# A two-layer hybrid backbone step on one core: loads of the start, modulation steps, the last RWKV pair and the odd projection's operands in another order

## Chip, cores and metric

The kernel runs on one core of a Trainium2 chip. The metric is the device time of one execution in microseconds (us).

## What is computed

The program is one inference step of a diffusion backbone of two layers, on 256 prompt tokens and 1024 sample tokens, 1024 features wide. Every sub-layer is a norm with a shift and a scale, a mixer or an MLP, and a gated addition to x. The shifts, scales and gates (the modulation) are one product per layer of the two conditioning vectors with `mod_w`. The cut reference:

```python
def modulation(cond, w, b):            # per layer, 6 x 1024 columns
    return silu(cond) @ w + b          # shift, scale, gate of mixer and of MLP
for l in range(2):
    h = rmsnorm(x, norm_mix[l]) * (1 + scale) + shift
    if l == 0:   # gated DeltaNet (q, k, v after a conv and silu) beside a gated short conv
        y = concat(gdn(h), short_conv(h)) @ ev_w_out
    else:        # windowed attention with sinks beside RWKV-7, forwards and backwards
        y = concat(attention(h), rwkv(h)) @ od_w_out
    x = x + gate * y
    h = rmsnorm(x, norm_mlp[l]) * (1 + scale2) + shift2
    x = x + gate2 * (relu(h @ mlp_w1) ** 2 @ mlp_w2)
out = rmsnorm(x, norm_final)
# end of the RWKV head, per pair of heads:
#   (groupnorm(y) * ln_w + ln_b + sum(r * k * r_k) * v) * g
```

## The kernel before

All activations lie feature by token: x is 8 tiles of 128 features by 1280 tokens. A dense product keeps fp32 accuracy through a split of both operands into a high and a low part (`split`: the high part on ACT, L247; the low part on POOL, L251, or on DVE, L253) and three TensorE products for each 128 by 128 block (`dense_mm`, L275). A column block of 128 outputs goes over the tokens in three chunks, CHUNKS = 256, 512 and 512 tokens wide, and over 8 feature blocks, so one chunk takes 24 matmuls. `load_w` loads a weight column block into a `raw` buffer (SP's queue, L263) and splits it into `whl`.

A scheduler with its own model of time sets the order in which each engine runs its instructions; the code below gives it the dependences. `late(a, b)` adds a dependence without a semaphore: a stands behind b in the order. `paced` does the same for matmuls that are to fill gaps of a serial chain. A DMA is issued by the queue of SP, ACT or POOL in that queue's order, and at most eight lanes are in use: a DMA waits for the lane that was given out eight DMAs earlier.

The places that matter here:

- **Start** (end of `tile_kernel`). `load_vec(1, SY, const)` loads eight small parameter rows on SP's queue (L185), among them the conditioning vectors, from which `scp` is made (L292 to L294). `load_x` loads the tokens on ACT's queue (L464), TensorE turns them (L151). `mod_set` (L300) loads 32 pieces of `mod_w` on SP's queue (L304), multiplies them (L305) and turns the result (L312). `norm` makes hhi and hlo (L454, L455). `spill_x` writes x to device memory (L126), eight DMAs on SP's queue.
- **Even mixer.** `qkv(h, i)` is one dense column block with a conv, a tanh (L619) and, for k and q, squares (ACT L630, POOL for the prompt) whose sums TensorE makes (L635). After each chunk `go_on(3)` takes three steps of the layer's other 16 groups of modulation columns: ACT multiplies a loaded piece (L357), POOL adds (L361), DVE folds (L367), TensorE sums the partitions (L373). The order was `qkv(0, 1)`, the small column block `ba` (L702, L711), then `qkv(0, 0)` and `qkv(0, 2)`.
- **MLP 0.** Layer 1's modulation is made beside the MLP, on DVE (L350).
- **Odd mixer.** Eight units of RWKV (four pairs b of heads, two directions d), each a serial chain `recur`, are filled up with attention items; `prep` of the next unit (its buffers come from the pool `rmore` on some turns, L1575) and `finish` of the pair before are spread over the same slot. `finish` has five parts: load r and the two k (L1806), mean and variance of Y (L1808 to L1818), the bonus (L1819, L1820), v and g (L1822, L1823), turn Y (L1827), sum the bonus (L1829), affine (L1831), gate (L1835) and write to `sp_w` (L1838). For the last pair all of it stands behind the last chain.
- **Odd projection.** `unspill_x` loads x in 24 DMAs on ACT's queue (L131). `odd_out` loads eight operands of 128 by 1280 (four of attention from `sp_a`, four of RWKV from `sp_w`) into two buffers `a` (L1849), and splits them; `project` runs the dense blocks db 7 to 4, chunk by chunk, then 3 to 0, and adds to x (L1866).

## Time and profile before

| | |
|---|---|
| Median of 3 runs | 4275.2 us (4267.73 to 4288.86) |
| Profiled execution, its own time | 4277.4 us |
| Its span, first to last instruction | 4275.4 us |
| Busy: PE, DVE, ACT, POOL | 3933.8, 2285.1, 1285.4, 1300.8 us |
| Mean granted TensorE clock | 0.944 of full speed |
| Stages (starts): start, even mixer, MLP 0, odd mixer, projection, MLP 1 | 0, 69, 1010, 1900, 3184, 3376 us |

PE is busy for 92% of the span; it is idle for the other 341 us. A wait is read with the engine that had it, the line that waited and the releaser: "PE pm L635 <- ACT t L630: 12.7" says that TensorE stood 12.7 us before its product of line 635, until ACT had written t at line 630.

### The profile page before, as it was taken

To read this page: it belongs to the slowest core of one execution; us is meant where nothing else is said; L and a number is where in the kernel's file an instruction comes from. 1 tells how busy PE (TensorE), PEld (TensorE's weight loads), DVE (VectorE), ACT (ScalarE), POOL (GpSimd) and SP (SyncE) were. 2 spreads that over 40 slices of the span, in tenths; PEclk is the share of its full clock that TensorE was granted. 3 is DMA by queue.
4 is the path that set the end of the run, shared out by engine and by line. 5 is a ranking of instruction groups with operands and counts; after the bars stand their busy time and mean duration, and the time that the engine had idled before them with its cause. 6 is when DMAs were issued, how large, how long until landed. Compare 5 with 4: busy or idle time off the path is not lost. (4 is left out here: it accounts for less than half of the span.)

```text
span 4275.4 us, 68726 instructions
## 1 busy us (share of the span) xinstructions
PE 3933.8 (92%) x27295; PEld 3228.1 (76%) x27295; DVE 2285.1 (53%) x4799; ACT 1285.4 (30%) x2721; POOL 1300.8 (30%) x1139
## 2 busy tenths in 40 slices
PE   6889989998999999999889889999868899999999
PEld 3677877786888888877667667777647788888887
DVE  5377676546455555463365577778541533333335
ACT  4454543223111111143222234444321311111112
POOL 2444542224222332242432231212022323322232
PEclk8889999999999999999989889999879999999999
DMA  5323332332122222125466543333242111111111
GB/s 206 101 81 100 93 98 70 126 131 73 53 75 72 71 79 75 47 98 181 147 211 185 137 101 82 91 88 82 64 134 67 30 40 40 40 35 35 40 40 60
DMA packets 437952, 382.90 MB, mean 90 GB/s; under 512 B 125684, under 2 KB 373503, under 8 KB 437503
## 3 DMA queue, kind: packets, MB, share of 16 engines
q1 hardware_dynamic: 405802, 314.45, 25.0%
q10 hardware_dynamic: 31829, 64.06, 4.5%
q8 instruction: 215, 3.52, 0.3%
q14 instruction: 106, 0.87, 0.1%
HBM read 290.31 MB, written 88.08 MB: 89 GB/s over the span
## 5 line engine op out<-in xcount | busy, mean ns | idle before, releaser
L275 PE MATMUL pd<-hhi,whl 128*128 128x512 f32 (+1 forms) x5376 | 1538.8, 366 | 55.0 <-ACT hhi L247 25.3
L275 PEld LDWEIGHTS pd<-hhi,whl 128*128 128x128 f32 x5376 | 974.9, 193 | 213.4 <-ACT hhi L247 27.1
L275 PE MATMUL pd<-hlo,whl 128*128 128x512 f32 (+1 forms) x2688 | 986.0, 367 | 27.1 <-POOL hlo L251 13.4
L512 DVE SCALAR_TENSOR_TENSOR x<-pm,mods,x 128x512 f32<-128x512 f32 (+1 forms) x768 | 501.7, 659 | 724.9 <-PE pm L511 724.7
L251 POOL TENSOR_TENSOR whl<-raw,whl 128x1024 fp32r<-128x1024 f32 (+1 forms) x203 | 471.2, 2331 | 611.3 <-ACT whl L247 610.1
L275 PEld LDWEIGHTS pd<-hlo,whl 128*128 128x128 f32 x2688 | 518.1, 193 | 115.3 <-DVE hlo L455 19.2
L509 PE MATMUL pm<-hh,whl 128*128 128x512 f32 (+1 forms) x1536 | 545.7, 356 | 0.0
L510 PE MATMUL pm<-hl,whl 128*128 128x512 f32 (+1 forms) x1536 | 544.4, 354 | 0.0
L511 PE MATMUL pm<-hh,whl 128*128 128x512 f32 (+1 forms) x1536 | 542.9, 354 | 0.0
L498 ACT ACTIVATE t<-pd 128x512 f32<-128x512 f32 (+1 forms) x192 | 101.1, 528 | 1307.6 <-PE pd L275 1305.3
L251 POOL TENSOR_TENSOR hl<-t,hh 128x512 fp32r<-128x512 f32 (+1 forms) x192 | 217.6, 1134 | 822.5 <-DVE hh L249 802.5
L509 PEld LDWEIGHTS pm<-hh,whl 128*128 128x128 f32 x1536 | 288.9, 188 | 44.5
L510 PEld LDWEIGHTS pm<-hl,whl 128*128 128x128 f32 x1536 | 289.4, 188 | 43.5
L511 PEld LDWEIGHTS pm<-hh,whl 128*128 128x128 f32 x1536 | 289.5, 188 | 41.7
L249 DVE CAST hh<-t 128x512 fp32r<-128x512 f32 (+1 forms) x192 | 164.0, 855 | 228.4 <-ACT t L499 228.3
L247 ACT ACTIVATE whl<-raw 128x1024 fp32r<-128x1024 f32 (+1 forms) x203 | 201.7, 1011 | 162.8 <-PE pm L511 74.7
L361 POOL TENSOR_TENSOR acc<-acc,modw 128x512 f32<-128x512 f32 x112 | 152.3, 1360 | 151.9 <-ACT modw L357 132.4
L357 ACT ACTIVATE modw<-modw,scp 128x256 f32<-128x256 f32 x224 | 113.0, 506 | 67.3 <-DMA modw<-in_mod_w_dram 61.9
L1276 PE MATMUL pa<-hst,whl 128*128 128x512 f32 (+1 forms) x432 | 121.1, 380 | 9.5 <-DMA hst<-sp_h 8.5
L350 DVE SCALAR_TENSOR_TENSOR acc<-modw,scp,acc 128x512 f32<-128x512 f32 x168 | 129.1, 800 | 0.2 <-DMA modw<-in_mod_w_dram 0.2
L284 PE MATMUL pd<-hhi,whl 128*128 128x512 f32 (+1 forms) x384 | 109.2, 364 | 4.9 <-ACT hhi L247 3.0
L420 ACT ACTIVATE sq<-x 128x512 f32<-128x512 f32 (+1 forms) x120 | 66.2, 558 | 157.3 <-DVE x L1866 48.0
(388 smaller groups left out, 5989.8 us busy)
## 6 DMA issues: line engine op xcount, KB each, us to landing
raw<-in_mlp_w_dram SPq DMA_DIRECT2D x128, 512.0 KB
modw<-in_mod_w_dram SPq DMA_DIRECT2D x128, 256.0 KB
hst<-sp_h ACTq DMA_DIRECT2D x48, 512.0 KB
modw<-in_mod_w_dram SPq DMA_DIRECT2D x128, 128.0 KB
rkk<-sp_r SPq DMA_DIRECT2D x40, 384.0 KB
raw<-in_ev_w_in_dram SPq DMA_DIRECT2D x28, 512.0 KB
x_dram<-x SPq DMA_DIRECT2D x16, 640.0 KB
x<-x_dram ACTq DMA_DIRECT2D x32, 256.0 KB
```

The source lines that it names most:

```text
L247: A.activation(out=hi, in_=src, func=AF.Copy)
L249: V.tensor_copy(out=hi, in_=src)
L251: G.tensor_tensor(out=lo, in0=src, in1=hi.bitcast(F32), op=ALU.subtract)
L275: paced(PE.matmul(ps[:, :N], w, x[:, t0:t0 + N], start=(n + i == 0), stop=(n == KB - 1 and i == 2)), N / 2400)
L350: V.scalar_tensor_tensor(out=acc[:, s], in0=w, scalar=scp[:, kb, s:s + 1], in1=acc[:, s], op0=ALU.mult, op1=ALU.add)
L357: bi = A.activation(out=dst[:, s], in_=w[:, 0], func=AF.Copy, scale=scp[:, kb, s:s + 1])
L361: G.tensor_tensor(out=acc, in0=acc, in1=w, op=ALU.add)
L509: PE.matmul(ps[:, :N], wh, hh[:, b, :N], start=(b == 0), stop=False)
L510: PE.matmul(ps[:, :N], wh, hl[:, b, :N], start=False, stop=False)
L511: PE.matmul(ps[:, :N], wl, hh[:, b, :N], start=False, stop=(b == 1))
L512: V.scalar_tensor_tensor(out=xt[db][:, t0:t0 + N], in0=ps[:, :N], scalar=gate[:, db, s:s + 1], in1=xt[db][:, t0:t0 + N], op0=ALU.mult, op1 ...
L1276: burst([(lambda w_=w_, i=i, w=w, h=h: PE.matmul(st["ps"][w_][:, :N], st["w"][w_][:, w, kb, :], x[:, h, :N], start=(kb + i == 0), stop=(kb ...
```

## The change

Six things are changed.

1. The small rows of `load_vec(1)` and the making of `scp` go into `conditions()`, on ACT's queue behind the first two loads of x. SP's queue begins with `mod_w`. The eight spills of x are kept behind the last load of `mod_w`.
2. `qkv(0, 1)` and `qkv(0, 0)` both come before `ba`; `ba`'s operands get buffers of their own. The first nine calls of `go_on` take no step of the modulation, each later one takes four.
3. In MLP 0 the DVE steps of layer 1's modulation are kept behind the latest eviction of the MLP (`late`, no semaphore).
4. `prep`'s extra buffers serve turns 9, 10 and 11 of each 11 instead of 1, 2 and 3.
5. For the last RWKV pair, bonus and gate are made `ahead`, in the last unit's slot, and written to `sp_e`; `rest` loads them again and does what needs Y.
6. `odd_out` loads each operand into the place of its own low part, in the order 0, 1, 2, 4, 5, 6, 3, 7, the last in three chunks, all on SP's queue and ahead of x, and splits there. The products take the feature blocks in the same order, and for db 7 to 4 the 256 tokens of the prompt come last. `unspill_x` is gone before the projection.

```diff
-    def spill_x(xt):
+    def spill_x(xt, after=None):
         for kb in range(KB):
-            SY.dma_start(out=x_dram[kb], in_=xt[kb])
+            dma = SY.dma_start(out=x_dram[kb], in_=xt[kb])
+            if after is not None:
+                late(dma, after)
...
-    load_vec(1, SY, const)
...
+    def conditions():
+        load_vec(1, A, const)
+        V.memset(scp, 0.0)
...
+                    late(bi, state["evict"])
                     yield
...
-            def go_on(n):
-                for _ in range(n):
-                    next(steps, None)
-
-            qkv(0, 1)
-            raw = state["raw"].tile([P, KB, 16], F32, tag="raw", name="raw")
+            def go_on():
+                if next(calls) >= 9:
+                    for _ in range(4):
+                        next(steps, None)
+
+            for i in (1, 0):
+                qkv(0, i)
+            raw = ge.tile([P, KB, 16], F32, tag="D1", name="rawb", bufs=1)
...
-            for i in (0, 2):
-                qkv(0, i)
+            qkv(0, 2)
...
-                    if u >= 7:
-                        pace["used"] = max(pace["used"], start - 0)
+                if u == 7:
+                    pre, last = finish(b)
+                    slot = [f for k, f in enumerate(slot) for f in ([f, pre.pop(0)] if k % 4 == 3 and pre else [f])] + pre
+                    pace["used"] = max(pace["used"], start)
...
-                g = state["more"] if state["more"] and turn[0] % 11 in (1, 2, 3) else gp
+                g = state["more"] if state["more"] and turn[0] % 11 in (9, 10, 0) else gp
...
+            def ahead(c0):
+                vg = tp.tile([P, 3, 256], F32, tag="vg", name="vg", bufs=1)
+                for _ in bonus(c0, vg):
+                    pass
+                ps = ps_t("pa")
+                paced(PE.matmul(ps[:, 256:], C["bd"], vg[:, 1], start=True, stop=True), 0.5)
+                paced(PE.matmul(ps[:, :256], ups[:, 2, :], vg[:, 2], start=True, stop=True), 0.5)
+                V.tensor_tensor(out=vg[:, 0], in0=vg[:, 0], in1=ps[:, 256:], op=ALU.mult)
+                A.activation(out=vg[:, 1], in_=ps[:, :256], func=AF.Copy)
+                SY.dma_start(out=mid["e"][:, :, 64 * c0:64 * c0 + 256], in_=vg[:, 0:2])
+
+            def rest(c0):
...
+                SY.dma_start(out=eg[:, 0:2], in_=mid["e"][:, :, sl])
+                head_norm(Yt)
+                ps = ps_t("pa")
+                by_feature(ps, Yt)
+                affine(eg[:, 2], ps)
+                G.tensor_tensor(out=eg[:, 2], in0=eg[:, 2], in1=eg[:, 0], op=ALU.add)
+                V.tensor_tensor(out=eg[:, 2], in0=eg[:, 2], in1=eg[:, 1], op=ALU.mult)
+                SY.dma_start(out=mid["w"][b][:, sl], in_=eg[:, 2])
...
-            for j in range(KB):
-                a = gp.tile([P, T], F32, tag="a", name="a", bufs=2)
-                (SY if j % 2 else A).dma_start(out=a, in_=mid["a"][j] if j < 4 else mid["w"][j - 4])
-                split(hs[j][0], hs[j][1], a, "a", "v" if j % 2 else "g")
+            def operand(j, sl, eng_lo):
+                hi, lo = hs[j][0][:, sl], hs[j][1][:, sl]
+                dma = SY.dma_start(out=lo.bitcast(F32), in_=(mid["a"][j] if j < 4 else mid["w"][j - 4])[:, sl])
+                split(hi, lo, lo.bitcast(F32), "a", eng_lo)
+                return dma
+
+            for j in (0, 1, 2, 4, 5, 6, 3):
+                last = operand(j, slice(0, T), "v" if j in (2, 5) else "g")
+            first = SY.dma_start(out=xt[7], in_=x_dram[7])
+            late(first, last)
+            for t0, N, s in (CHUNKS[1], CHUNKS[2], CHUNKS[0]):
+                last = operand(7, slice(t0, t0 + N), "v")
+            for kb in range(KB - 2, -1, -1):
+                late(SY.dma_start(out=xt[kb], in_=x_dram[kb]), last)
...
-            project(e2, xt, hs, cols, gate, range(KB))
+            project(e2, xt, hs, cols, gate, (0, 1, 2, 4, 5, 6, 3, 7))
...
-            for c in CHUNKS:
+            for c in (CHUNKS[1], CHUNKS[2], CHUNKS[0]):
...
         load_x(xp_, xt, (2, 4))
+        conditions()
...
-        spill_x(xt)
+        spill_x(xt, state["last"])
...
-    unspill_x(xt)
     odd_out(xt, hs, mod_gate(1, 0))
```

**SP at the start, before**, from the eighth small row to the last piece of `mod_w` (L304) and the two weight loads behind it. L126 are the spills of x, L702 is the load of `ba`'s weights.

```order
L185 DMA rows_74<-in_gdn_norm_dram 1x128
L304 DMA modw<-in_mod_w_dram 128x512 x17
L263 DMA raw<-in_ev_w_in_dram 128x8x128
L702 DMA raw<-in_ev_w_in_dram 128x8x16
L304 DMA modw<-in_mod_w_dram 128x512 x8
L126 DMA x_dram<-x 128x1280 x3
L304 DMA modw<-in_mod_w_dram 128x512 x2
L126 DMA x_dram<-x 128x1280 x4
L304 DMA modw<-in_mod_w_dram 128x512 x4
L126 DMA x_dram<-x 128x1280
L304 DMA modw<-in_mod_w_dram 128x512
L263 DMA raw<-in_ev_w_in_dram 128x8x128 x2
```

The same place in the changed program, from SP's first DMA on (L308 is the load of `mod_w` now, L709 that of `ba`):

```order
L145 DMA cst<-in_c_dram 128x896
L147 DMA cst_72<-in_c_dram 128x192
L308 DMA modw<-in_mod_w_dram 128x512 x11
L263 DMA raw<-in_ev_w_in_dram 128x8x128 x2
L308 DMA modw<-in_mod_w_dram 128x512 x10
L263 DMA raw<-in_ev_w_in_dram 128x8x128
L308 DMA modw<-in_mod_w_dram 128x512 x2
L263 DMA raw<-in_ev_w_in_dram 128x8x128
L308 DMA modw<-in_mod_w_dram 128x512 x9
L126 DMA x_dram<-x 128x1280 x8
L709 DMA rawb<-in_ev_w_in_dram 128x8x16
```

No spill and no load of `ba` stands among the 32 pieces any more; one weight load more does.

**ACT in the even mixer, before**, from the first tanh of `qkv(0, 1)` (L619) to the squares (L630); L357 are the modulation's products.

```order
L619 ACTIVATE t_807<-cv 128x512
L619 ACTIVATE t_827<-cv 128x512
L357 ACTIVATE modw<-modw,scp 128x256 x2
L574 ACTIVATE raw<-pd 128x256
L575 ACTIVATE cv<-pd,vec_83 128x256
L247 ACTIVATE whl<-raw 128x1024
L357 ACTIVATE modw<-modw,scp 128x256
L619 ACTIVATE t_845<-cv 128x256
L357 ACTIVATE modw<-modw,scp 128x256 x9
L630 ACTIVATE t_863<-cv 128x512
L630 ACTIVATE t_869<-cv 128x512
```

The same in the changed program (tanh L624, squares L635, products L362):

```order
L624 ACTIVATE t_807<-cv 128x512
L624 ACTIVATE t_810<-cv 128x512
L362 ACTIVATE modw<-modw,scp 128x256 x2
L579 ACTIVATE raw<-pd 128x256
L580 ACTIVATE cv<-pd,vec_197 128x256
L247 ACTIVATE whl<-raw 128x1024
L362 ACTIVATE modw<-modw,scp 128x256
L624 ACTIVATE t_813<-cv 128x256
L635 ACTIVATE t_818<-cv 128x512
L362 ACTIVATE modw<-modw,scp 128x256
L635 ACTIVATE t_824<-cv 128x512
```

The nine products that stood right ahead of the first square are gone from there; some products still stand in this stretch, since the scheduler puts them where it finds room.

**SP at the projection, before**, from the last writes of `sp_w` on; the other four operands and the 24 loads of x are on ACT's queue.

```order
L1838 DMA sp_w<-yT 128x256
L1849 DMA a<-sp_a 128x1280
L1849 DMA a<-sp_w 128x1280 x2
L263 DMA raw<-in_od_w_out_dram 64x4x128 x2
```

The same in the changed program (L1893 is the last write of `sp_w`, L1907 the operands, L1913 and L1918 x):

```order
L1893 DMA sp_w<-eg 128x256
L263 DMA raw<-in_od_w_out_dram 128x4x128
L1907 DMA hlo<-sp_a 128x1280 x3
L1907 DMA hlo<-sp_w 128x1280 x3
L1907 DMA hlo<-sp_a 128x1280
L1913 DMA x<-x_dram 128x1280
L1907 DMA hlo<-sp_w 128x512
L1907 DMA hlo<-sp_w 128x256
L1907 DMA hlo<-sp_w 128x512
L1918 DMA x<-x_dram 128x1280 x7
```

All operands now stand in one queue, seven of them ahead of any load of x.

## Rows read from the trace of the kernel before

**Rows 1.** Stretches: us, then busy us of PE, PEld, DVE, ACT, POOL; clock, DMA share, GB/s.

```profile
0.00:70.00 70.00, 42.87 (x192) 21.16 (x192) 23.61 (x62) 21.92 (x52) 12.19 (x15) 0.88 0.85 304
...
1030.00:1800.00 770.00, 770.00 (x4037) 650.62 (x4037) 416.58 (x652) 140.04 (x219) 226.57 (x138) 1.00 0.22 67
...
3185.00:3240.00 55.00, 26.85 (x92) 20.49 (x93) 11.15 (x7) 11.00 (x9) 13.99 (x5) 0.71 0.50 168
```

**Rows 2.** Timeline of SP's queue: the first pieces of mod_w (start, us, line, DMA).

```profile
10.74 1.30 SPq L304 DMA_DIRECT2D modw<-in_mod_w_dram  x3
```

**Rows 3.** DMA of 0 to 64 us: GB/s in 40 slices, total, issues (KB each).

```profile
GB/s 0 255 392 404 418 256 8 173 331 274 319 411 413 378 310 236 289 286 367 408 412 345 168 112 339 300 265 375 416 422 412 399 428 435 419 401 394 412 371 348
DMA packets 11402, 20.96 MB, mean 328 GB/s; under 512 B 1970, under 2 KB 4870, under 8 KB 11398
...
modw<-in_mod_w_dram SPq DMA_DIRECT2D x32, 256.0 KB
x_dram<-x SPq DMA_DIRECT2D x8, 640.0 KB
xs<-in_x_sample_dram ACTq DMA_DIRECT2D x4, 1024.0 KB
raw<-in_ev_w_in_dram SPq DMA_DIRECT2D x3, 512.0 KB
```

**Rows 4.** Timeline of PE, 63 to 70 us (idle before and its releaser in brackets).

```profile
63.93 1.04 PE L305 MATMUL pm<-modw,scp 128*32 128x512 f32 x2 [0.28 <-DMA modw<-in_mod_w_dram]
...
69.36 0.79 PE L275 MATMUL pd<-hhi,whl 128*128 128x512 f32 x1 [2.01 <-ACT hhi L454]
```

**Rows 5.** Timeline of POOL, 44 to 70 us: the norm's factor of the last tokens.

```profile
47.84 0.71 POOL L406 TENSOR_TENSOR rs<-ms,mhalf 128x2 f32<-128x2 f32 x1 [2.29 <-DVE ms L427]
```

**Rows 6.** Waits of PE, 100 to 300 us: total, times, longest.

```profile
PE pm L635 <- ACT t L630: 13.3, 2, 12.7
PE pm L373 <- DVE acc L367: 10.7, 2, 8.4
```

**Rows 7.** Timeline of ACT, 112 to 113 us, ahead of the squares.

```profile
112.18 1.05 ACT L357 ACTIVATE modw<-modw,scp 128x256 f32<-128x256 f32 x2 [4.84 <-DMA modw<-in_mod_w_dram]
```

**Rows 8.** Timeline of SP's queue at the ends of units 1, 2 and 3 (L1795).

```profile
2501.68 0.34 SPq L1795 DMA_DIRECT2D out_dram<-so  x1
...
2644.06 0.36 SPq L1795 DMA_DIRECT2D out_dram<-so  x1
...
2751.33 0.62 SPq L1795 DMA_DIRECT2D out_dram<-so  x1
```

**Rows 9.** Waits of PE, 3140 to 3186 us.

```profile
PE pa L1829 <- DVE vg L1820: 7.5, 3, 3.5
```

**Rows 10.** Timeline of all engines, 3169 to 3202 us: from the last chain to the first product.

```profile
3169.64 1.12 PE L1766 MATMUL pc<-SH,AR 64*64 64x64 f32 x16
...
3175.44 0.61 POOL L1818 TENSOR_TENSOR Yt<-Yt,rst 128x256 f32<-128x256 f32 x1
...
3184.68 0.32 SPq L1838 DMA_DIRECT2D sp_w<-yT  x1
...
3200.86 1.43 PE L275 MATMUL pd<-hhi,whl 128*128 128x512 f32 x3 [17.26 <-ACT hhi L247]
```

**Rows 11.** Groups by shape, 3180 to 3240 us, and DVE's last low part there.

```profile
L251 POOL TENSOR_TENSOR hlo<-a,hhi 128x1280 fp32r<-128x1280 f32 x4 | 11.6, 2900 | 34.6 <-ACT hhi L247 29.7 <-DMA a<-sp_w 4.8
L251 POOL TENSOR_TENSOR whl<-raw,whl 128x1024 fp32r<-128x1024 f32 x1 | 2.4, 2393 | 6.0 <-ACT whl L247 6.0
...
3230.33 1.49 DVE L253 TENSOR_TENSOR hlo<-a,hhi 128x1280 fp32r<-128x1280 f32 x1 [6.37 <-ACT hhi L247]
```

**Rows 12.** DMA of 3184.7 to 3231 us, total and mean rate; ACT's queue: an operand's way.

```profile
DMA packets 4455, 9.30 MB, mean 201 GB/s; under 512 B 496, under 2 KB 1648, under 8 KB 4454
...
3222.64 0.33 ACTq L1849 DMA_DIRECT2D a<-sp_w  x1
3226.11 1.27 ACT L247 ACTIVATE hhi<-a 128x1280 fp32r<-128x1280 f32 x1 [3.77 <-DMA a<-sp_w]
```

More of the change, by code (lines that the diff above doesn't have):

```diff
@@ L288, in tile_kernel @@
     cvec = const.tile([P, 2, KB], F32, name="cvec")
-    V.memset(scp, 0.0)
-    for s, nm in enumerate(("c_ctx", "c")):
-        th = cvec[:, s, :]
-        A.activation(out=th, in_=vec[nm], func=AF.Tanh, scale=0.5)
-        V.scalar_tensor_tensor(out=th, in0=th, scalar=1.0, in1=vec[nm], op0=ALU.add, op1=ALU.mult)
-        V.tensor_scalar(out=scp[:, :, s], in0=th, scalar1=0.5, scalar2=None, op0=ALU.mult)
+    def conditions():
+        load_vec(1, A, const)
+        V.memset(scp, 0.0)
+        for s, nm in enumerate(("c_ctx", "c")):
+            th = cvec[:, s, :]
+            A.activation(out=th, in_=vec[nm], func=AF.Tanh, scale=0.5)
+            V.scalar_tensor_tensor(out=th, in0=th, scalar=1.0, in1=vec[nm], op0=ALU.add, op1=ALU.mult)
+            V.tensor_scalar(out=scp[:, :, s], in0=th, scalar1=0.5, scalar2=None, op0=ALU.mult)
     mods = [const.tile([P, 48, 2], F32, name=f"mods{l}") for l in range(2)]
@@ L303, in mod_set @@
                 c0 = u * D + 512 * j
-                SY.dma_start(out=w, in_=I["mod_w"][l, kb * P:(kb + 1) * P, c0:c0 + 512])
+                state["last"] = SY.dma_start(out=w, in_=I["mod_w"][l, kb * P:(kb + 1) * P, c0:c0 + 512])
                 PE.matmul(ps[64 * j:64 * j + 32, :], scp[:, kb, :], w, start=(kb == 0), stop=(kb == KB - 1),
@@ L1097, in odd_mixer @@
         sp_w = dram.tile([4, P, T], F32, name="sp_w")
-        mid.update(a=sp_a, w=sp_w)
+        sp_e = dram.tile([P, 2, T], F32, name="sp_e")
+        mid.update(a=sp_a, w=sp_w, e=sp_e)
         mid_tap = const.tile([P, 15], F32, name="mid_tap")
@@ L1347, in odd_mixer @@
                     ends.pop(0)()
-                if d == 1:
+                if d == 1 and b < 3:
                     ends = finish(b)
-            for f in ends:
+            for f in last:
                 f()
@@ L1800, in finish, with bonus, head_norm @@
             bcol = lambda t: t.rearrange("p (c o) -> p c o", o=1).to_broadcast([P, 4, 64])
-            def part(c0):
-                Yt = live.pop(("Y", b, c0 // 4))
+            def bonus(c0, vg):
                 sl = slice(64 * c0, 64 * c0 + 256)
-                vg = tp.tile([P, 3, 256], F32, tag="vg", name="vg", bufs=1)
                 for i, src in enumerate((sp_r[b][:, 0, sl], sp_k2[b % 2, 0][:, sl], sp_k2[b % 2, 1][:, sl])):
                     SY.dma_start(out=vg[:, i], in_=src)
+                yield
+                G.tensor_tensor(out=vg[:, 1], in0=vg[:, 1], in1=vg[:, 2], op=ALU.add)
+                V.scalar_tensor_tensor(out=vg[:, 1], in0=vg[:, 1], scalar=vec["r_k"][:, b:b + 1], in1=vg[:, 0],
+                                       op0=ALU.mult, op1=ALU.mult)
+                SY.dma_start(out=vg[:, 0], in_=sp_v[b][:, sl])
+                SY.dma_start(out=vg[:, 2], in_=sp_g[:, sl])
+            def head_norm(Yt):
                 mean = sp.tile([P, 4], F32, tag="gn", name="mean", bufs=4)
@@ L1818, in part, with by_feature @@
                 G.tensor_tensor(out=Yt, in0=Yt, in1=bcol(rst), op=ALU.mult)
[L1819 to L1824 removed]
+            def by_feature(ps, Yt):
                 for c in range(4):
@@ L1828, in part, with affine @@
                                   start=True, stop=True)
+            def affine(yT, ps):
+                A.activation(out=yT, in_=ps[:, :256], func=AF.Identity, scale=vec["ln_w"][:, b:b + 1],
+                             bias=vec["ln_b"][:, b:b + 1])
+            def part(c0):
+                Yt = live.pop(("Y", b, c0 // 4))
+                vg = tp.tile([P, 3, 256], F32, tag="vg", name="vg", bufs=1)
+                steps = bonus(c0, vg)
+                next(steps)
+                head_norm(Yt)
+                next(steps, None)
+                ps = ps_t("pa")
+                by_feature(ps, Yt)
                 PE.matmul(ps[:, 256:], C["bd"], vg[:, 1], start=True, stop=True)
                 yT = tp.tile([P, 256], F32, tag="yT", name="yT", bufs=1)
-                A.activation(out=yT, in_=ps[:, :256], func=AF.Identity, scale=vec["ln_w"][:, b:b + 1],
-                             bias=vec["ln_b"][:, b:b + 1])
+                affine(yT, ps)
                 V.tensor_tensor(out=vg[:, 0], in0=vg[:, 0], in1=ps[:, 256:], op=ALU.mult)
@@ L1837, in part @@
                 V.tensor_tensor(out=yT, in0=yT, in1=pg[:, :256], op=ALU.mult)
-                SY.dma_start(out=mid["w"][b][:, sl], in_=yT)
-            return [lambda c0=c0: part(c0) for c0 in (16, 0, 12, 8, 4)]
+                SY.dma_start(out=mid["w"][b][:, 64 * c0:64 * c0 + 256], in_=yT)
+            order = (16, 0, 12, 8, 4)
+            def ahead(c0):
+                vg = tp.tile([P, 3, 256], F32, tag="vg", name="vg", bufs=1)
+                for _ in bonus(c0, vg):
[7 more added lines that the diff above has]
+            def rest(c0):
+                Yt = live.pop(("Y", b, c0 // 4))
+                sl = slice(64 * c0, 64 * c0 + 256)
+                tg = EG[order.index(c0)]
+                eg = tp.tile([P, 4, 3, 64] if tg == "BK" else [P, 3, 256], F32, tag=tg, name="eg", bufs=1 if tg == "vg" else 2)
+                if tg == "BK":
+                    eg = eg.rearrange("p a b q -> p (a b q)").rearrange("p (a q) -> p a q", q=256)
+                SY.dma_start(out=eg[:, 0:2], in_=mid["e"][:, :, sl])
+                head_norm(Yt)
+                ps = ps_t("pa")
+                by_feature(ps, Yt)
+                affine(eg[:, 2], ps)
+                G.tensor_tensor(out=eg[:, 2], in0=eg[:, 2], in1=eg[:, 0], op=ALU.add)
+                V.tensor_tensor(out=eg[:, 2], in0=eg[:, 2], in1=eg[:, 1], op=ALU.mult)
+                SY.dma_start(out=mid["w"][b][:, sl], in_=eg[:, 2])
+            EG = ("rkk", "rkk", "BK", "BK", "vg")
+            if b < 3:
+                return [lambda c0=c0: part(c0) for c0 in order]
+            return [lambda c0=c0: ahead(c0) for c0 in order], [lambda c0=c0: rest(c0) for c0 in order]
         return prep, recur, finish
```

29 lines of the change are left out of this document (11 added, 18 removed).

## The prediction

> **What bounds the kernel.** I read the stretches first, to see where TensorE is not busy. In MLP 0 it is busy for 770 of 770 us; at the start for 42.87 of 70 us, and in the first 55 us of the projection for 26.85 of 55 [rows 1]. The reader is to see there that the change works where TensorE has idle time, except for its third part. Then I read what TensorE waits for in each of these places. At the start it is the DMA traffic: the DMA engines are busy for 0.85 of the stretch at 304 GB/s [rows 1], the last pieces of `mod_w` are multiplied at 63.93 us and the first dense product starts at 69.36 us [rows 4]. In the even mixer two waits stand out, 13.3 us for the squares and 10.7 us for a modulation sum [rows 6]. At the end of the odd mixer the last write of `sp_w` is issued at 3184.68 us, and the first product of the projection begins 16.2 us later [rows 10].
>
> The sum is made against the profiled execution's own 4277.4 us, 2.2 us above the median of the runs. The measurement can tell a change of about 0.5%, 21.4 us, from none.
>
> **1. Start.** SP issues its first piece of `mod_w` at 10.74 us [rows 2], since eight small rows stand ahead of it; in the slices from 9.6 to 12.8 us the DMA engines move 8 and 173 GB/s [rows 3]. The change puts 11 pieces first. The spills, 8 x 640 KB = 5.24 MB [rows 3], stood between the pieces and go behind them. What has to land before the last piece is then 32 x 256 KB of `mod_w`, 5 x 1024 KB of x, four weight loads of 512 KB and some 0.6 MB of constants: 8.39 + 5.24 + 2.10 + 0.6 = 16.3 MB. At 350 GB/s, a rate between the mean of 328 and the 412 that many slices show [rows 3], that is 47 us, and 2 us before the first bytes: 49. At 328 it is 52, at 412 it is 42. The way from the last piece to the first dense product took 69.36 - 63.93 = 5.4 us [rows 4] and stays. So the first product would start at 54.4 instead of 69.36, 15 us earlier. I take 1 us off: `scp` is made behind more work on ACT, and SP's pieces wait for buffers until TensorE has used the first 11. **14 us** gained. The low end is 7: the norm's last factor came at 47.84 us [rows 5], and with x and `mod_w` sharing the engines from the first microsecond it can come up to 8 us later and become what is waited for. The high end is 20. The small rows go to ACT's queue, where they stand between copies of x; what they cost there is inside these ends. The `ba` weights come behind the spills: 5.24 MB at 350 GB/s are 15 us, so about 66 us, ahead of the split that needs them, which stands behind the whole norm on ACT.
>
> **2. Even mixer.** In front of the squares ACT ran nine products with modulation pieces and waited for their loads, 4.84 us once [rows 7]; TensorE stood 12.7 us behind them [rows 6]. In the new order two of them are left between the tanhs and one between the squares, and a whole column block more of dense products stands ahead of the sums of squares on TensorE. That wait should go. The steps return later, four per call instead of three, and there the waits for a modulation sum, 10.7 us [rows 6], have the same cause and can move rather than vanish. Best case both go, 24 us gained. Worst case, the first one only moves and the second grows by a third, 4 us, and the recurrence, which has 72 dense products beside its second step where it had 132, loses some 5: 9 us lost. I take **10 us** gained, nearest to the row of the wait that the order removes, less a share that comes back.
>
> **3. MLP 0.** TensorE is never idle there [rows 1]. The DVE steps moved behind evictions have that whole stretch as cover: **0**. If the cover were gone, a step delayed past its MLP block would show as TensorE idle in this stretch, and there is none to price it by; I allow 3 us either way.
>
> **4. Extra buffers on other turns.** `prep` of unit 3 has the extra ones no longer, and its last two groups wait until unit 2 frees its own. In unit 2, which ran without extra buffers, the distance between ends is 2644.06 - 2501.68 = 142.4 us, in unit 3 with them 107.3 [rows 8]. So up to 35 us of distance can be moved to unit 3. But the attention items fill TensorE in these slots, and what is not used in one is used in a later one, as long as items are left. I take **0**, with -12 and +12 as ends: a third of that distance either way.
>
> **5. Last pair.** From the last product of the chain, ending at 3170.76 us, to the last write of `sp_w` it is 13.9 us [rows 10], of which the parts with the bonus make most: the second part's turned Y is ready at 3176 us, and the rest waits for r, k and the bonus. In the new order the path from the chain is: sum and turn of Y as before to 3175.44 + 0.61, 5.3 us behind the chain; a weight's low part that stands in POOL's order between, 2.39 us [rows 11]; a turn, an affine and a second low part beside them, 2.4 us; the addition and the product with their handoffs, 1.2 us: 11.3, so 2.6 us gained. The three waits of TensorE for the bonus, 7.5 us together [rows 9], 4 of them ahead of the chain's end, lie in the chain's own order and go: 4 us more. The work itself, five times the loads, one POOL and two DVE instructions and two products, moves into the last unit's slot, where attention items cover it; it adds five writes and five loads of 256 KB. **7 us** gained, with +12 and -3 as ends: -3 if it stretches the chain by one more wait of that row's length.
>
> **6. Operands.** Before, 24 loads of x stand ahead, and the first high part is made after them; the last low part ends at 3231.82 us [rows 11], 47.1 us behind the last write of `sp_w`. Now an operand's way from issue to its high part is 3.5 us, and the high part takes 1.27 [rows 12]. Five low parts follow one another on POOL at 2.9 us each [rows 11]: 3.5 + 1.3 + 14.5 = 19.3 us. The loads of eight operands and x[7], 5.9 MB, take 18 us at 328 GB/s, and the last chunk's split stands behind them: 21 us. So the slower of the two is 21, against 47.1: **26 us** gained; both ways end within 2 us of each other, so neither is much of a lever alone. Behind the last operand the products follow as before, and the remaining seven column blocks were already without waits. At the mean rate of that stretch, 201 GB/s [rows 12], the loads take 29 us and the gain is 15; with the prompt's short chunk last, 2.4 us less remain behind the last operand, and the gain is up to 31. The loads of x for the other blocks now come behind the operands; the first is due when db 7 is done, and x[7] is ahead of the last.
>
> **Sum.** 14 + 10 + 0 + 0 + 7 + 26 = 57 us: 4277.4 - 57 = **4220 us**.
>
> **Rivals.**
> *A, the start stays bound by the bytes.* The pieces come earlier and x later by as much, the norm ends late, and the first product gains only 4 us. For it: the engines are busy for 0.85 of the stretch [rows 1], and the norm's last factor is only 16 us ahead of the last piece [rows 4, 5]. Against it: 5.24 MB leave the stretch and the dip is 300 GB/s deep. Time: 4230. The Trainium skill, page "DMA: Bandwidth & Descriptors", section "Issuing engines are not separate DMA queues", speaks for this one: it says that DMAs of several issuing engines run on the same 16 DMA engines and interleave, so that another queue saves only the time of issuing. The busy share of that stretch agrees, the dip does not.
> *B, the even mixer or the units lose what the start gains.* The waits of part 2 come back whole, and the buffers of part 4 cost their 12 us: 10 + 12 less gained, 4242; with the worst of part 2 it is 4251. For it: the modulation's steps are denser, and two waits of rows 6 have them as releaser. Against it: the order shows the nine products gone.
> *C, the operands come by the mean rate*, because the weights and x[7] share the engines: 11 us less, 4231.
> *D, slower: unit 3's buffers hold up every chain behind.* The place is `prep` of unit 3, whose last two groups wait for unit 2's buffers. If the units that draw on the changed turns, 3 and 4, each take unit 2's distance instead of unit 3's, 2 x 35 = 70 us are lost [rows 8], and attention is spent before it can fill the later slots: 4220 + 70 = 4290. It decides from 57 us of lost distance on. Against it: the units behind share fills of attention that are the same in number.
> *E, the change does not do what it says.* The scheduler places the modulation by its own clock, and three products still stand ahead of the second square; if the wait stays there, only part 2 falls away: 4230. It is counted with B.
>
> **Chances.** All terms near their values: 0.62, with 4200 to 4240 as its own range. A 0.12, C 0.08, B with E 0.13, D 0.05. Likeliest 4220. The range of 8 in 10 takes in A, C and most of B, and on the other side the high ends of parts 1 and 6, 6 + 5 us, and half of part 2's, 7: low 4196 with the rest, high 4254. Faster by over 0.5% means under 4253.8: all but D and a part of B and of what I have not thought of, 0.86; within 0.5%: 0.09; slower by over 0.5%: 0.05.
>
> **What would show it.** Right, if the first dense product starts near 54 us; no wait of 12 us for the squares near 90 us; the idle time of TensorE between the last `sp_w` write and the first product near 5 us, and the first eviction of the projection some 26 us closer to that write. Part 4 is wrong if the units' ends drift apart by over 12 us in 3 or 4, part 2 if new waits for modulation sums of over 10 us stand after 200 us. The whole is wrong if the loads of the operands queue behind weights or x, so that low parts still end 35 us or more behind `sp_w`.

## The result, and the profile after

The changed kernel takes 4230.3 us, median of 4 runs (4218.0 to 4232.1), against 4279.9 for the kernel before, run beside it: ratio 0.9884, 95% interval [0.9858, 0.9910], 49.6 us less. Forecast were 4220 and a gain of 57. The profiled execution has a span of 4226.4 us, and its stages say that the right total is made of terms of which three lay outside their own ranges and happened to cancel.

The page of the changed kernel, part 1 and the rows of TensorE and of its clock from part 2:

```profile
span 4226.4 us, 68798 instructions
...
PE 3917.9 (93%) x27295; PEld 3217.3 (76%) x27295; DVE 2285.1 (54%) x4800; ACT 1287.8 (30%) x2728; POOL 1304.5 (31%) x1140
...
PE   6989899999999999989889889899769899999999
...
PEclk8989999999999999999989799999889999999999
```

TensorE's busy time is 16 us less with the same number of matmuls, and its idle time 33 less (308 us, from 341). Its mean granted clock is 0.952, from 0.944.

Where the two executions stand at the same places of the program (us from the span's start):

| place | before | changed | earlier by |
|---|---|---|---|
| first dense product | 69.4 | 66.8 | 2.6 |
| last eviction of the even projection | 971.0 | 951.2 | 19.8 |
| first eviction of MLP 0 | 1017.5 | 986.8 | 30.7 |
| end of RWKV unit 0 | 2373.8 | 2341.6 | 32.2 |
| end of unit 2 | 2644.1 | 2608.6 | 35.4 |
| end of unit 4 | 2858.4 | 2850.3 | 8.0 |
| end of unit 7 | 3158.7 | 3139.2 | 19.5 |
| last write of sp_w | 3184.7 | 3156.1 | 28.6 |
| last eviction of the odd projection | 3334.7 | 3284.0 | 50.7 |
| end | 4275.4 | 4226.4 | 49.0 |

Differences of the right column are the terms: start 2.6 (forecast 14), even mixer 17.2 (10), norm ahead of MLP 0 10.9 (0), units 0 to 7 -12.7 (0), last pair 9.1 (7), operands 22.1 (26). What lies between the first eviction of MLP 0 and unit 0 and behind the projection makes +1.5 and -1.7. An eviction is the instruction that adds a finished block of a product to x.

**Start.** Timelines of the changed kernel, of TensorE, then of SP's queue, then of ACT and its queue:

```profile
26.82 6.61 PE L309 MATMUL pm<-modw,scp 128*32 128x512 f32 x20 [8.85 <-DVE scp L297]
...
61.58 1.05 PE L309 MATMUL pm<-modw,scp 128*32 128x512 f32 x2
...
66.77 0.79 PE L275 MATMUL pd<-hhi,whl 128*128 128x512 f32 x1 [2.01 <-ACT hhi L459]
...
1.65 14.04 SPq L308 DMA_DIRECT2D modw<-in_mod_w_dram  x11
15.99 1.53 SPq L263 DMA_DIRECT2D raw<-in_ev_w_in_dram  x2
29.28 5.35 SPq L308 DMA_DIRECT2D modw<-in_mod_w_dram  x10
...
4.58 0.52 ACTq L187 DMA_DIRECT2D rows<-in_norm_final_dram  x1
10.59 0.30 ACTq L187 DMA_DIRECT2D rows<-in_gdn_conv_dram  x1
...
25.02 0.29 ACT L295 ACTIVATE cvec<-vec 128x8 f32<-128x8 f32 x2
```

The norm's factor of the last tokens (POOL) and the last load of x (ACT's queue) in the changed kernel, then that load and the first modulation product in the kernel before; the factor of before is in [rows 5]:

```profile
59.85 0.71 POOL L411 TENSOR_TENSOR rs<-ms,mhalf 128x2 f32<-128x2 f32 x1 [1.93 <-DVE ms L432]
37.27 0.40 ACTq L469 DMA_DIRECT2D xs<-in_x_prompt_dram  x1
...
25.59 0.40 ACTq L464 DMA_DIRECT2D xs<-in_x_prompt_dram  x1
16.79 1.04 PE L305 MATMUL pm<-modw,scp 128*32 128x512 f32 x2 [0.25 <-DVE scp L294]
```

The stretch from the first to the last modulation product in the changed kernel (columns as in [rows 1]):

```profile
26.80:62.60 35.80, 32.01 (x152) 13.50 (x152) 13.84 (x31) 13.93 (x31) 11.43 (x9) 0.94 0.89 316
```

The pieces of `mod_w` start at 1.65 us instead of 10.74 [rows 2], but the small rows on ACT's queue stand from 5.1 to 10.6 us, for the lane that the second load of x had been given, and the tanh of the conditions comes at 25 us. So `scp` is there at 26.8 us, 10 later than before. SP's queue has filled the 11 buffers and stops from 17.5 to 29.3 us. From `scp` on TensorE is busy for 32.0 of 35.8 us: modulation products and the turns of x behind them. The last product ends at 62.6 us, 2.3 earlier than the 65.0 of before [rows 4]. With the turns, x came later too: its last load is issued 11.7 us later, and the norm's last factor is made at 59.9 us instead of 47.8, now nearly at the same time as the last product.

**Units.** Timeline of POOL in the changed kernel, the first instruction of three groups of `prep` for unit 3, and SP's queue at unit 2's end and at unit 3's inverse (rbi), which its chain needs:

```profile
2545.69 0.92 POOL L1587 TENSOR_TENSOR AR<-rkk,px 128x256 f32<-128x256 f32 x1 [9.29 <-PE pc L1775]
2566.64 0.92 POOL L1587 TENSOR_TENSOR AR<-rkk,px 128x256 f32<-128x256 f32 x1 [3.62 <-PE pc L1775]
2587.41 0.94 POOL L1587 TENSOR_TENSOR AR<-rkk,px 128x256 f32<-128x256 f32 x1 [4.10 <-PE pc L1775]
...
2608.62 0.38 SPq L1804 DMA_DIRECT2D out_dram<-so  x1
2622.32 0.32 SPq L1629 DMA_DIRECT2D rbi<-sub  x1
```

Group after group waits until a product of unit 2's chain (L1775) frees a buffer, about 20 us apart. The inverse of unit 3 is written 13.7 us after unit 2's end; in the kernel before, 45.5 us ahead of it (2644.06 in [rows 8]):

```profile
2598.54 0.32 SPq L1620 DMA_DIRECT2D rbi<-sub  x1
```

**Last pair and operands.** Timelines of the changed kernel from the last chain to the low parts:

```profile
3144.25 1.12 PE L1775 MATMUL pc<-SH,AR 64*64 64x64 f32 x16
...
3156.13 0.60 SPq L1893 DMA_DIRECT2D sp_w<-eg  x1
3156.77 0.43 SPq L263 DMA_DIRECT2D raw<-in_od_w_out_dram  x1
3158.74 1.29 SPq L1907 DMA_DIRECT2D hlo<-sp_a  x3
...
3164.07 1.43 PE L275 MATMUL pd<-hhi,whl 128*128 128x512 f32 x3 [10.41 <-ACT hhi L247]
3164.10 17.48 POOL L251 TENSOR_TENSOR hlo<-hlo,hhi 128x1280 fp32r<-128x1280 f32 x5 [8.62 <-ACT hhi L247]
...
3167.23 15.23 DVE L253 TENSOR_TENSOR hlo<-hlo,hhi 128x1280 fp32r<-128x1280 f32 x5 [11.29 <-ACT hhi L247]
```

The groups of the low parts by shape, 3156 to 3185 us:

```profile
L251 POOL TENSOR_TENSOR hlo<-hlo,hhi 128x1280 fp32r<-128x1280 f32 x5 | 17.5, 3530 | 8.6 <-ACT hhi L247 8.6
...
L253 DVE TENSOR_TENSOR hlo<-hlo,hhi 128x1280 fp32r<-128x1280 f32 x2 | 8.2, 4132 | 11.3 <-ACT hhi L247 11.3
...
L253 DVE TENSOR_TENSOR hlo<-hlo,hhi 128x256 fp32r<-128x256 f32 x1 | 3.1, 3142 | 0.0
```

From the chain's last product, ending at 3145.4, to the last write it is 10.8 us (13.9 before). The first product of the projection starts 7.9 us behind that write, not 16.2 [rows 10], and the last low part ends at 3182.5, 26.3 us behind it, not 47.1.

### The profile page after: what moved, and what is told of

Its sections match the earlier page's. It is cut to its first block, busy times and chain, and to the rows that moved or that the text cites. A ratio compares the mean times of both kernels' runs of the same rounds, so it can differ in the third digit from the quotient of the medians.

```text
span 4226.4 us, 68798 instructions
## 1 busy us (share of the span) xinstructions
PE 3917.9 (93%) x27295; PEld 3217.3 (76%) x27295; DVE 2285.1 (54%) x4800; ACT 1287.8 (30%) x2728; POOL 1304.5 (31%) x1140
## 5 line engine op out<-in xcount | busy, mean ns | idle before, releaser
L249 DVE CAST hh<-t 128x512 fp32r<-128x512 f32 (+1 forms) x192 | 134.9, 703 | 193.6 <-ACT t L504 193.6
L354 DVE SCALAR_TENSOR_TENSOR acc<-modw,scp,acc 128x512 f32<-128x512 f32 x168 | 162.9, 969 | 0.0
L362 ACT ACTIVATE modw<-modw,scp 128x256 f32<-128x256 f32 x224 | 112.6, 506 | 86.8 <-DMA modw<-in_mod_w_dram 83.7
```

What stands on the lines that cost most here:

```text
L249: V.tensor_copy(out=hi, in_=src)
L354: bi = V.scalar_tensor_tensor(out=acc[:, s], in0=w, scalar=scp[:, kb, s:s + 1], in1=acc[:, s], op0=ALU.mult, op1=ALU.add)
L362: bi = A.activation(out=dst[:, s], in_=w[:, 0], func=AF.Copy, scale=scp[:, kb, s:s + 1])
```

## The experiments

Each starts from the changed kernel, if nothing else is said. Single stages are compared in profiled executions, one for each kernel. How far these repeat: the last eviction of the even projection comes at 951.2, 954.8 and 956.6 us in the three kernels with the same TensorE order up to there (the changed one, h_spill, u5_bonus), and at 952.9, 954.3 and 956.1 in three that have a few instructions otherwise (u6_operands, u4_turns, u3_evict). So differences of some 5 us at that place say nothing, and the changed kernel's execution is the earliest of the six.

**First part undone (u1_start).**

```diff
-    def conditions():
-        load_vec(1, A, const)
-        V.memset(scp, 0.0)
+    load_vec(1, SY, const)
+    V.memset(scp, 0.0)
...
-        conditions()
...
-        spill_x(xt, state["last"])
+        spill_x(xt)
```

> The changed kernel with its first part undone (small rows on SP's queue ahead of mod_w, spills free to stand between its pieces). In the changed kernel the first dense product started at 66.8 us, only 2.6 earlier than before, since scp was ready at 26.8 us instead of 16.8. Theory A, the first part as it stands is worth those 2.6 us and no more: first dense product near 69 us, everything behind it as in the changed kernel, about 4233. Rival B, the order of the first loads also helps the even mixer behind it (four weights loaded early, ba late): the first GDN state is then also later by 8 us or more against the first dense product, 4240 or more.

4253.0 us, ratio to the kernel before 0.9946 [0.9930, 0.9962]. First dense product at 70.5 us, last even eviction at 973.4 instead of 951.2: 3.7 us at the start and 18.5 behind it. Rival B. Those 18.5 are spread, as the stretch between the two places shows for the changed kernel, then for this one (columns as in [rows 1]):

```profile
66.77:951.20 884.43, 803.06 (x5313) 670.66 (x5314) 545.11 (x1315) 387.40 (x888) 344.18 (x305) 0.95 0.33 99
```

```profile
70.52:973.42 902.90, 812.12 (x5313) 679.12 (x5314) 546.58 (x1315) 389.53 (x888) 342.98 (x305) 0.93 0.32 97
```

TensorE is busy for 812.1 us against 803.1, at a granted clock of 0.93 against 0.95, and idle for 90.8 against 81.4; no single wait grew by more than 3.2 us. Of the first 5700 instructions on TensorE some 600 stand in another order, though no line of the even mixer was edited. That the scheduler planned with other arrival times is a guess.

**Only the spills' place undone (h_spill):** `spill_x(xt)` again, the rest of the first part kept.

> The changed kernel with only the order of the spills undone (they may stand between the pieces of mod_w). The first part as a whole was worth 22 us at the last even eviction, 3.7 of them at the first dense product. Theory A, the place of the spills does it, since they hold SP's queue and the bytes: first dense product 3 us or more later, last even eviction near 973 instead of 951, about 4250. Rival B, the place of the small rows and of ba does it: both within 4 us of the changed kernel, about 4230.

4240.9 us, 0.9913 [0.9893, 0.9933]; first dense product at 67.2, last even eviction at 954.8. Rival B for these stages, where TensorE's order is that of the changed kernel (up to 2201 us). So the spills alone do not make the loss of u1_start there; it takes the small rows in their old place, alone or together with the spills, and no run tells these two apart. The median is 10 us above, with runs from 4229 to 4251 that overlap; that part stays open.

**Second part undone (u2_qkv).**

```diff
-                if next(calls) >= 9:
-                    for _ in range(4):
-                        next(steps, None)
+                for _ in range(3):
+                    next(steps, None)
-            for i in (1, 0):
-                qkv(0, i)
+            qkv(0, 1)
...
-            qkv(0, 2)
+            for i in (0, 2):
+                qkv(0, i)
```

> The changed kernel with its second part undone (qkv order, three modulation steps per call from the first call on, ba's shared buffers). Theory A, the second part is worth what the stretch from the first dense product to the last GDN state gained, 17 us: TensorE waits 10 us or more for the squares again, last GDN state 15 to 20 us later, about 4247. Rival B, the gain came from the loads of the start, which this kernel keeps: no wait of 10 us, within 5 us of 4230.

4238.1 us, 0.9913 [0.9898, 0.9928]. Waits of TensorE in this kernel, 68 to 330 us:

```profile
PE pm L640 <- ACT t L635: 13.3, 2, 12.7
PE pm L378 <- DVE acc L372: 8.5, 2, 6.1
```

In the changed kernel, 100 to 300 us, the first is short and the second is not there:

```profile
PE pm L640 <- ACT t L635: 2.2, 1, 2.2
```

Both waits of [rows 6] are back, the first at its old 13.3 us, and the last even eviction is at 972.5, 21 us later. Theory A in mechanism. In the whole only 8 us are lost; in the profiled execution units 0 to 7 take 781.6 us here against 797.6. Together with u1_start it says more: with one of the two parts alone the even projection ends at 972.5 and 973.4, with neither at 971.0, with both at 951.2. They don't add up: either alone gave nothing at that place, and the 22 us are well above the 5 or so by which it varies.

**Third part undone (u3_evict):** the line `late(bi, state["evict"])` taken out.

> The changed kernel with its third part undone (no dependence of the DVE modulation steps on MLP evictions). In the kernel before, DVE ran 14 such steps, 12.3 us, between the instructions of the norm ahead of MLP 0; in the changed one none stands there, and the way from the last product of the even projection to MLP 0's first eviction is 11 us shorter. Theory A: those steps are the cause, they return there and the way grows by 9 to 12 us, about 4241. Rival B, the norm got shorter by another order that has nothing to do with them: the way stays within 3 us, about 4230.

4248.2 us, 0.9932 [0.9918, 0.9947]. From the last even eviction to MLP 0's first it takes 47.6 us, against 35.6: theory A, 12 us. In all twelve kernels that have the part it takes 32.6 to 35.6 us, in the two without it 46.5 and 47.6. The stretch between the two in the kernel before, in the changed kernel and in this one (columns as in [rows 1]):

```profile
971.00:1017.50 46.50, 31.51 (x116) 23.71 (x115) 36.82 (x55) 19.84 (x37) 25.98 (x15) 0.78 0.32 100
```

```profile
951.20:986.80 35.60, 30.58 (x122) 24.00 (x121) 24.86 (x38) 19.57 (x37) 21.38 (x16) 0.88 0.23 71
```

```profile
956.10:1003.70 47.60, 34.83 (x118) 26.22 (x117) 37.50 (x54) 19.50 (x37) 23.29 (x15) 0.73 0.32 98
```

DVE's busy time is what changes, 36.8 to 24.9 and back to 37.5 us: the modulation steps between the norm's own. In the kernel before, 971 to 1017.5 us, DVE's costliest group is such steps; in the changed kernel none is in the stretch:

```profile
L350 DVE SCALAR_TENSOR_TENSOR acc<-modw,scp,acc 128x512 f32<-128x512 f32 x14 | 12.3, 887 | 0.0
```

MLP 0 itself got shorter as well. Its evictions in the changed kernel, then in this one (first and last start):

```profile
L517 DVE SCALAR_TENSOR_TENSOR x<-pm,mods,x x384: 472/745/754, 986.8 to 1865.2; 128x512 f32<-128x512 f32 x128, 128x256 f32<-128x256 f32 x64
```

```profile
L516 DVE SCALAR_TENSOR_TENSOR x<-pm,mods,x x384: 468/746/754, 1003.7 to 1886.1; 128x512 f32<-128x512 f32 x128, 128x256 f32<-128x256 f32 x64
```

That is 878.4 us against 882.4, which is also what the kernel before took; in the eleven other kernels with the part it is 878.4 to 878.6. TensorE is busy for all but 3 us of the stretch either way, so why it takes 4 us more is not shown. Of the 18 us of the medians 16 are found in these two places.

**Fourth part undone (u4_turns).**

```diff
-                g = state["more"] if state["more"] and turn[0] % 11 in (9, 10, 0) else gp
+                g = state["more"] if state["more"] and turn[0] % 11 in (1, 2, 3) else gp
```

Distance n is, as in the prediction, the time from the end of unit n-1 to that of unit n; distances 3 and 4 were 107.3 and 107.0 us before and are 125.5 and 116.2 in the changed kernel.

> The changed kernel with the extra buffers back on turns 1, 2 and 3. In the changed kernel the distances of unit ends 3 and 4 were 125.5 and 116.2 us against 107.3 and 107.0 before, and from the end of unit 0 to that of unit 7 it took 12.7 us longer. Theory A, the turns are the cause: distances 3 and 4 go back to 107 to 112, the stretch from unit 0 to unit 7 shrinks by 10 to 16 us, 4215 to 4220. Rival B, the fill of the slots is the cause (bonus ahead, another order of attention items): distances stay within 4 us of the changed kernel's, about 4230.

4221.0 us, 0.9872 [0.9855, 0.9888]; distances 3 and 4 are 113.0 and 106.0, and from unit 0 to unit 7 it takes 775.6 us, 22 less. POOL's groups and the inverse of unit 3 in this kernel:

```profile
2538.76 0.88 POOL L1587 TENSOR_TENSOR AR<-rkk,px 128x256 f32<-128x256 f32 x1 [1.68 <-ACT px L1570]
2564.00 0.71 POOL L1587 TENSOR_TENSOR AR<-rkk,px 128x256 f32<-128x256 f32 x1 [1.71 <-ACT px L1570]
...
2565.61 0.32 SPq L1629 DMA_DIRECT2D rbi<-sub  x1
2614.80 0.34 SPq L1804 DMA_DIRECT2D out_dram<-so  x1
```

No group of unit 3 waits for the chain, and the inverse is there 49 us ahead of the end of unit 2. Theory A, with more than its 10 to 16 us between the units; 6.5 us of that are lost again behind unit 7. Over all profiles of this study, units 0 to 7 take 775.6 to 784.9 us with turns 1 to 3 (five kernels) and 781.6 to 827.2 with turns 9 to 11 (nine). The intervals of the two medians overlap here, so for this pair the gain is read from the stages. Two more pairs below differ in the turns alone: c_first and best1 (4258.1 and 4220.7 us, intervals apart) and c_early4 and best4 (4221.2 and 4214.2, intervals overlapping). The old turns are the faster ones in all three.

**Fifth part undone (u5_bonus):** `finish` of the last pair in five whole parts behind the last chain.

> The changed kernel with its fifth part undone (the last pair's bonus and gate behind the last chain again). Theory A, from the end of unit 7 to the last write of sp_w it takes 26 us again instead of 16.9, 9 us more, about 4239, and units 5 and 6 stay within 5 us. Rival B, the work ahead also costs its place in the last slot: distances 5 to 7 shrink by 5 us or more, so that the whole is within 4 us of 4230.

4231.7 us, 0.9906 [0.9884, 0.9928]. Behind unit 7's end it takes 26.2 us, as theory A says (16.9 in the changed kernel); but distance 7 is 79.8 us instead of 91.7, as rival B says, and the median is unchanged. The time behind the chain is moved into the slot in front of it: distance 7 and what follows it make 106.0 us here and 108.6 in the changed kernel.

**Sixth part undone (u6_operands):** `unspill_x` and the old `odd_out`, blocks and chunks in the old order.

> The changed kernel with its sixth part undone (24 loads of x first, operands in two buffers, feature blocks and chunks in the old order). In the changed kernel it is 127.9 us from the last write of sp_w to the projection's last eviction, 150.0 before. Theory A: 148 to 152 again, about 4252. Rival B, part of that came from the shorter tail of part 5: 135 to 145.

4255.8 us, 0.9948 [0.9931, 0.9966]. From the last write of `sp_w` to the last eviction it takes 155.5 us, against 127.9: theory A, somewhat above its range. The part is worth 25 us in the medians, the most of the six, though its interval overlaps those of u1_start (23 us) and u3_evict (18 us). What the six lose one by one makes 66 us, more than the whole gain of 50: the parts are not independent.

**Can the start be had? (c_first, c_early4).** c_first puts the two conditioning rows into a group of their own, first on ACT's queue.

> The changed kernel with the two conditioning rows in a group of their own, first on ACT's queue behind two loads of x, and the other small rows behind the two tanh instructions. In the changed kernel scp is ready at 26.8 us, SP's queue stands from 17.5 to 29.3 us with all 11 buffers full, and the DMA rate falls to 3 GB/s in one slice. Theory A, the late scp is what took the start's gain: scp ready by 13 us, no stop of SP's queue of more than 4 us ahead of the last piece of mod_w, first dense product at 55 to 60 us, 7 to 12 us gained there, about 4220. Rival B, the bytes bound the start: scp early, but the first dense product within 3 us of 66.8.

4258.1 us, 0.9957 [0.9941, 0.9973]; `scp` at 19.3 us, first dense product at 65.5. The kernel doesn't test what it was made for: TensorE's order put the turns of later tokens and of the other small rows ahead of the products, so they began at 31.9 us only, and units 0 to 7 took 827 us in another order. c_early4 fixes TensorE's order by `late`:

```diff
-        load_vec(1, A, const)
+        load_vec(3, SY, const)
...
+                        if c0 in (6, 8, 0):
+                            late(bi, state["mm"][{6: 9, 8: 15, 0: 21}[c0]])
...
+        if gi in (0, 1):
+            late(bi, state["mm"][9])
...
+                if state["nw"] in (3, 4):
+                    late(dma, state["last"])
```

Group 3 holds c_ctx and c, on SP's queue ahead of `mod_w`; `mm` lists the modulation products, and the turns of x and of the small rows stand behind some of them; `nw` counts the weight loads.

> The changed kernel with the two conditioning rows on SP's queue ahead of mod_w, the other small rows behind the tanhs, the later turns of x and the turns of the small rows behind the first modulation products on TensorE, and the third and fourth weight load behind the last piece of mod_w. Theory A: in the changed kernel TensorE itself bounds the start, since from the moment scp is ready, 26.8 us, it is busy for 32.0 of the 35.8 us up to the last modulation product; with scp at 16 us or earlier and the products right behind it, the first dense product comes at 55 to 60 us instead of 66.8, and the last even eviction of x, 951 us, 7 to 12 us earlier if the even mixer keeps its order. Rival B, the bytes bound the start: first dense product within 3 us of 66.8 though scp is early. Rival C, the start gains but the even mixer's order comes out worse, as when either of the first two parts is undone: the last even eviction is not earlier than 951.

4221.2 us, 0.9867 [0.9850, 0.9883]. Timeline of TensorE in it:

```profile
17.75 7.15 PE L318 MATMUL pm<-modw,scp 128*32 128x512 f32 x22
30.91 1.87 PE L441 MATMUL pn<-cst,sq 128*128 128x2 f32 x8 [6.00 <-DVE sq L438]
...
62.31 0.74 PE L284 MATMUL pd<-hhi,whl 128*128 128x512 f32 x1 [0.19 <-ACT hhi L470]
```

The products start 9.1 us earlier, the first dense product 4.5: in between TensorE waits 6 us for the squares of x. The norm's factor of the last tokens in it:

```profile
60.93 0.71 POOL L422 TENSOR_TENSOR rs<-ms,mhalf 128x2 f32<-128x2 f32 x1 [3.21 <-DVE ms L443]
```

Half of A, short of its 55 to 60 us: the edit gave back some 4 us, and what the first dense product then waits for is x itself, since the norm's last factor is made only 1.4 us ahead of it. The last even eviction is at 955.1, no earlier than in the changed kernel, which fits rival C, though a gain of 4 us could not be told there; the median's 9 us lie inside the overlap of the intervals.

**A faster version (best1, best4, best5).** best1 is c_first with the turns back, best4 is c_early4 with the turns back, best5 is best4 with the fifth part undone.

> The conditioning rows first and the extra buffers back on turns 1, 2 and 3, together, on the changed kernel. If both act by themselves, the sum: 7 to 12 us from the start and 10 to 14 from the units, 4205 to 4213, and faster than the changed kernel beyond the interval of the measurement. If the scheduler's new order gives one of them back, 4215 to 4225.

4220.7 us, 0.9876 [0.9857, 0.9895]: the second expectation, in which one of the two is given back.

> The same with the extra buffers back on turns 1, 2 and 3. If both act by themselves: 7 to 12 us from the start and 8 to 14 from the units, 4205 to 4215. If the orders of the scheduler give one of them back: 4215 to 4225.

4214.2 us, 0.9850 [0.9836, 0.9865], the lowest median of all, 16 us below the changed kernel's median; the runs of the two (4209.4 to 4216.6, 4218.0 to 4232.1) don't overlap, the intervals of the two ratios just do, so that it is the faster one is likely and not shown. First dense product at 61.0, last even eviction at 952.3, units 0 to 7 in 783.1 us.

> The fastest of these kernels (conditioning rows first on SP, modulation products ahead of later turns, extra buffers on turns 1, 2 and 3; 4214 us) with the fifth part undone too, so that the last pair's bonus stands behind the last chain. Theory A, from the run in which the fifth part alone was undone: what it saves behind the last chain, 9 us, its work in the last slot costs again, so the median stays within 4 us of 4214. Rival B, it saves what stands behind the chain: about 4223, with 26 us from unit 7's end to the last write of sp_w and distance 7 unchanged at 85.

4217.5 us, 0.9861 [0.9838, 0.9883]. Unit 7's end to the last write is 26.8 us against 23.4 in best4, distance 7 82.2 against 84.9: theory A, the fifth part gives and takes about the same.

## Why the prediction was right, and where not

- **Part 1, start: 14 forecast, 2.6 measured.** The step that failed is "I take 1 us off: `scp` is made behind more work on ACT". It took 10 us more, and the sum of bytes left out what TensorE has to do behind `scp`, 32 us. A second step failed with it: the norm's last factor "can come up to 8 us later", and it came 12 later. c_early4 gave 4.5 us back and then waited for that norm. Rival A was near in number (4 us) and right that x comes later and the norm ends late; that the bytes bound it is not what the trace shows, since the DMA rate falls to 14 GB/s in one slice while SP waits for buffers. The Trainium skill, page "DMA: Bandwidth & Descriptors", section "Issuing engines are not separate DMA queues", would have taken the small rows' move for little; the trace agrees that it gained little in transfers (319 GB/s over the first 64 us, 328 before [rows 3]), and it lost time on ACT.
- **Part 2, even mixer: 10 forecast, 17.2 measured**, and 11 to 17 over the six executions named above. The wait of 12.7 us went and came back when the part was undone, and the later sums no longer waited. What the step left out is that the first part decides it too: neither alone moved the end of the even projection. The reading of the new order was off by one, which bore on nothing: three products stand between the tanhs, not two.
- **Part 3: 0 forecast, 10.9 measured** up to MLP 0's first eviction and 14.9 up to its last. The step "TensorE is never idle there" is true of the stretch from 1030 us, and the steps that the edit moves do not begin there. DVE ran 14 of them, 12.3 us, between the norm's instructions, where MLP 0 waits for that norm. I had read the stretch in which the MLP runs instead of all places where the line runs. And that stretch itself got 4 us shorter though TensorE reads as busy in it either way: that it is never idle did not make the term nothing.
- **Part 4: 0 forecast, -12.7 measured for units 0 to 7.** The wait was named and its place was right (`prep` of unit 3 until unit 2 frees buffers). The step that failed is "what is not used in one is used in a later one": the loss of units 3 and 4, 27 us, was made good only in part. It is rival D's mechanism at a fifth of its price. The size is rough: nine kernels with the new turns spread over 46 us there.
- **Part 5: 7 forecast, 9.1 measured behind the chain**, but the slot that was to cover its work did not; undone, it changed no median.
- **Part 6: 26 forecast, 22.1 measured.** The form was right: operands first, two ways that end together. From the last write to the last low part 21 us were forecast and 26.3 measured. Mis-sized were the low parts, 3.5 us each on POOL for 2.9, and the first load, issued 2.6 us behind the write where none was counted.

So the total was right within 10 us by luck: -11 and -13 stood against +7, +11 and small terms.

## What to carry to other kernels

When instructions are moved, list every place where their line runs, not only the stage that the edit names; 14 of 168 outside it were worth 11 us here. When loads are moved forward, follow the smallest operand that the first consumer needs (`scp`, made from two rows of 4 KB), and count what the consumer has to do from then on, not only the bytes. Where a scheduler sets the order, two edits can be worth nothing apart and 20 us together at one place: measure them in all combinations.

## What was not expected of the hardware

A low part of 128 by 1280 on DVE took 4.13 us while POOL ran the same operation all the time, and one of 128 by 256, a fifth of the size, took 3.14. In the kernel before, two of DVE's four started while POOL's was running, the others at its end. These are POOL's second and DVE's second; DVE's fourth is in [rows 11]:

```profile
3211.51 2.90 POOL L251 TENSOR_TENSOR hlo<-a,hhi 128x1280 fp32r<-128x1280 f32 x1 [7.73 <-ACT hhi L247]
...
3212.63 3.13 DVE L253 TENSOR_TENSOR hlo<-a,hhi 128x1280 fp32r<-128x1280 f32 x1 [7.49 <-ACT hhi L247]
```

DVE's ends 1.35 us behind POOL's, about as long as DVE's fourth took by itself (1.49). So the two ran this operation one after the other, not side by side, and it is not the new place of the operand that made it slow. Estimated from these times, five low parts of 2.90 us and three of 1.35 one after another are 18.6 us; the eight operands of the changed kernel took 18.4, POOL's 3.53 each. The prediction had counted 14.5 us for POOL's five and no time of DVE's beside them; [rows 11] show only the one of DVE's four that hardly met POOL's.
